# The small matmuls of two mixers: keys in tiles of 72, 72 and 128, matmuls of one array shape side by side

## The chip, the cores and the metric

The kernel runs on one core of a Trainium2 chip. The metric is the time of the program on the device in microseconds (us), from runs of the whole program; a profiled execution of the same program gives the rows that are read below.

## What is computed

A trunk of two layers over 256 frames with 16 learned meta tokens ahead of them, so 272 tokens of 1024 features, all in float32. Every layer adds half a gated feed-forward network, a mixer, and half a second feed-forward network. The parts of the reference that matter here are the mixers:

```python
for layer in range(DEPTH):
    h = h + 0.5 * swiglu(rms_norm(h, ffn1_norm[layer]), ...)
    hn = rms_norm(h, mix_norm[layer])
    y = even_mixer(hn, ...) if layer % 2 == 0 else odd_mixer(hn, ...)
    h = h + y
    h = h + 0.5 * swiglu(rms_norm(h, ffn2_norm[layer]), ...)
return h[:, N_META:]

# even_mixer: 8 indexer heads score the keys, the 64 best keys of each query are kept,
#   8 heads of softmax attention over them; beside it retention with 8 heads:
score = einsum('bqh,bqhs->bqs', iwb, relu(einsum('bqhd,bsd->bqhs', iqb, ik)))
s = einsum('bqhd,bqkhd->bhqk', qb, kg) * dh ** -0.5      # masked, softmax, times v
inner = einsum('bnihd,bnjhd->bnhij', qc, kc) * dmat      # retention: masked, times v
# odd_mixer: 8 heads of windowed attention (2 key heads) with one more score, the sink;
#   beside it a causal mean over 2, 4, 8 and 16 tokens through a 128x128 matrix each
p = softmax(concatenate([s, sink], axis=-1), axis=-1)[..., :-1]
```

## The kernel before

**The stream.** All weights are cut into 128x128 blocks, 2680 of them, packed in the order of their use. Each block is loaded (L138), split into two parts `whi` and `wlo` by ScalarE (L156) and VectorE or GpSimd (L157), and used by three matmuls (`mmw`, L247 to L249) on a moving operand of 272 or 256 token columns. Blocks follow each other in fixed lists of groups (`EV_GROUPS`, `OD_GROUPS` and others); a group's blocks add up in one PSUM bank.

**The work beside it.** What a mixer does with a projection's result (norms, scores, softmax, products) is written as generators, called tasks. A task issues some instructions and yields a number: so many stream blocks are issued before its next step. These numbers stand in the table `W`. So the order on every engine is fixed when the program is built, and each engine takes its instructions in that order. In the mixers a unit of eight blocks is split in two halves of 128x512 (`halves`), one each four blocks.

**Tokens.** Tokens stand in columns, so 272 keys are cut as 128, 128 and 16. A query block is 128 of the 256 frames: the first (`t=0`) sees 144 keys, the second (`t=1`) all 272. Heads stand in pairs in one tile of 128 rows, head `p` on rows 64p to 64p+63.

**The small matmuls**, which are the ones that the change touches:
- The indexer (L573): for 8 heads and 2 query blocks one matmul of 64 rows each, then ScalarE's relu (L575) and VectorE's sum (L578).
- Attention (`attend`): one task for a head pair and a query block, 8 in each mixer. It issues the scores of both heads (L470), their maxima with the mask (L476, VectorE), the exponentials (L480, ScalarE), the division by the sum (L483, L485, VectorE), the turns of the probabilities through TensorE (L493, and L494 for the last 16 keys), copies (L498, L499), and the product with the values (L506, and L507 for the 16 keys) into rows 64p of one bank, head by head.
- Retention (`retain`), once for each of 8 heads: turn of the values (L668), scores (L675 to L677), masks (L680 to L682), and seven blocks later the product (L685 to L687).
- `head_norm` (L433, L436) is the norm of a head's queries or keys. In the odd mixer it waits 15 blocks (`hn_sum`) after the square on ScalarE (L433) before the sum over rows (L436). `norm_r` (L302) is the norm over all features; a mixer's first result waits for it. `pool_mix` (L809 on GpSimd, L813, L816, L819, L821) is the causal mean.

Float32 matmuls of the side work run as two passes; turns run as one. What TensorE's rows call `64*128` is the shape of the stationary operand: rows and columns of the array that the matmul uses.

Of the kernel before, what the change touches and what calls it, by code (L numbers as in the profile page):

```python
# [11 lines left out]
F32 = mybir.dt.float32  # L12
F32R = mybir.dt.float32r
AF = mybir.ActivationFunctionType
# [38 lines left out]
def order_ffn_in0():  # L53
    """The very first phase: in the order in which the tokens are loaded."""
# [13 lines left out]
OD_GROUPS = ([("ck", 0), ("cq", 0), ("cv", 0)] + [("cq", i) for i in (1, 2, 3)] + [("dx", i) for i in (3, 2, 1, 0)])  # L68
# [41 lines left out]
# How many blocks of the weight stream go between the steps of the work beside it.  # L110
W = dict(first_sq=2, hid=6, hid_lo=1, hn_sum=15, hn_out=15, tok=15, tok_out=1, ev=dict(max=1, exp=5, norm=2,
         turn=4, copy=5, pv=6, lo=1), ev_every=(11, 11), od=dict(max=1, exp=4, norm=1, turn=3, copy=1, pv=4,
         lo=1), od_every=(5, 8), ix=10, ix_add=2, top_a=5, top_b=3, meta=4, rope=10, ret_v=1, ret_s=1,
         ret_y=7, ret_sum=7, ret_out=14, ret_lo=2, pool=7, pool_g=8, pool_mm=4, pool_lo=4)


class Weights:
    """The stream of weight blocks: loaded, split into two float32r parts, and handed out in order."""
# [23 lines left out]
    def load_part(self, i):  # L142
        """The first unit in two loads."""
# [8 lines left out]
    def part(self, u, s):  # L152
        """Splits the columns s of unit u."""
# [48 lines left out]
class Trunk:  # L202
# [32 lines left out]
    def table(self, name):  # L235
        """Loads the activation tables of the functions that follow, where one set serves several of them."""
# [15 lines left out]
    def rsqrt(self, out, mean, on=None):  # L252
        """out = (mean + eps) ** -0.5: the table's value and one Newton step; mean may be in PSUM."""
# [16 lines left out]
    def prep_x(self, m, norm, c):  # L270
        """The moving operand of the next projection: h * gain in two float32r parts."""
# [9 lines left out]
    def finish(self, m, ps, coef, norm, c):  # L281
        """h += coef * ps, and what the next norm and projection need of it."""
# [15 lines left out]
    def norm_r(self, c):  # L298
        """The norm's factor per token, on every partition."""
# [9 lines left out]
    def start(self):  # L309
# [9 lines left out]
        # The tensor engine's clock rises once it has been busy for a while: it starts on zeros.  # L319
# [28 lines left out]
    def first_x(self):  # L348
        """The first norm's operand, and the sum of squares that it needs later."""
# [79 lines left out]
    def head_norm(self, raw, gain, pool, tag, bufs, put, c=slice(0, T)):  # L429
        """RMSNorm over the 64 dims of each of the two heads of a tile."""  # L430
# [3 lines left out]
        yield W["hn_sum"]  # L434
# [4 lines left out]
        yield W["hn_out"]  # L439
# [4 lines left out]
    def to_tokens(self, raw, put):  # L444
        """[128 dims, tokens] -> three tiles [tokens, 128 dims] through the tensor engine."""
# [3 lines left out]
        for i, n in ((0, 128), (1, 128), (2, 16)):  # L449
# [536 lines left out]
```

## Time and profile before

| | us |
|---|---|
| median of 3 runs | 1116.1 (1114.81 to 1116.37) |
| span of the profiled execution, first to last instruction | 1113.3 |
| TensorE busy in it | 1104.5 (99%) |
| VectorE busy | 712.1 (64%) |
| ScalarE busy | 523.9 (47%) |
| GpSimd busy | 172.0 (15%) |
| even mixer, its first stream matmul to the next phase's first | 229.9 |
| odd mixer, the same | 83.5 |

The profiled execution gives a span and no time of its own beside it; the runs lie 2.8 us above that span in the median. PE is TensorE's matmuls, PEld its weight loads, DVE VectorE, ACT ScalarE, POOL GpSimd, SP SyncE. A matmul's row has its start and its length; the length holds the way through the array (0.28 us for one of 272 columns, while the next starts 0.13 us after it), so the cost of something between stream matmuls is read from the starts around it.

### The profile page before, as it was taken

Reading aid. Unit: us, or ns where it says so; the run is one execution under the profiler, and the core shown is the slowest. Engines: PE = TensorE matmul, PEld = TensorE weight load, DVE = VectorE, ACT = ScalarE, POOL = GpSimd, SP = SyncE. Lnnn points to the kernel's source line nnn. Section 1 sums busy time; section 2 is a strip of 40 time slices with the busy share of each in tenths; the row PEclk is TensorE's granted clock in tenths of the full one; section 3 lists DMA queues with packets and bytes.
Section 4 is the critical chain, followed back from the end, with each engine's and each line's share of the span. In section 5 each row is a group of like instructions: output and inputs, shape, how many; then the busy total and the mean of one; then the engine's idle time right before and its main releaser. Section 6 shows DMA issues by size and latency. Waiting matters only on the chain.

```text
span 1113.3 us, 20774 instructions
## 1 busy us (share of the span) xinstructions
PE 1104.5 (99%) x8624; PEld 1064.0 (96%) x8624; DVE 712.1 (64%) x1244; ACT 523.9 (47%) x877; POOL 172.0 (15%) x213
## 2 busy tenths in 40 slices
PE   8999999999999999999999999999999999999998
PEld 7999999989889899999999999999999799999998
DVE  5776654559864567776664476665557867777642
ACT  6554434446345455544443354443435546554531
POOL 2000002428430444000001200000113421000000
PEclk9999999999999999999999999999999999999999
DMA  7554544424643225454545445545454225555551
GB/s 269 191 196 182 186 162 183 136 105 152 205 152 125 97 87 184 179 192 159 186 154 189 188 152 189 179 164 189 151 194 165 76 77 181 199 198 184 192 202 40
DMA packets 29533, 183.39 MB, mean 165 GB/s; under 512 B 3648, under 2 KB 6080, under 8 KB 8320
## 3 DMA queue, kind: packets, MB, share of 16 engines
q1 hardware_dynamic: 29184, 181.25, 45.3%
q8 instruction: 67, 1.10, 0.4%
q0 software_dynamic: 256, 0.83, 0.2%
q14 instruction: 26, 0.21, 0.1%
HBM read 179.90 MB, written 1.05 MB: 163 GB/s over the span
## 4 chain that ended last, share of the span: by engine, by line
PE 92%; DVE 5%; ACT 1%; DMA 1%; issue 0%; SPq 0%; DVEq 0%; ACTq 0%
PE mm L247 29%; PE mm L248 28%; PE mm L249 28%; DVE wlo L157 2%; PE sd L506 1%; PE sd L507 1%; PE sd L573 1%; PE sd L470 1%; PE sd L493 1%; DMA raw<-in_w 1%; ACT whi L156 1%; PE sd L675 0%; DVE ev_t L441 0%; DVE isc L587 0%; PE sd L668 0%
## 5 line engine op out<-in xcount | busy, mean ns | idle before, releaser
L247 PE MATMUL mm<-xhi,whi 128*128 128x272 f32 (+1 forms) x1816 | 532.7, 293 | 1.4 <-ACT whi L156 1.3
L249 PE MATMUL mm<-xhi,wlo 128*128 128x272 f32 (+1 forms) x1816 | 521.0, 287 | 1.2 <-DVE wlo L157 1.2
L248 PE MATMUL mm<-xlo,whi 128*128 128x272 f32 (+1 forms) x1816 | 520.6, 287 | 0.2
L157 DVE TENSOR_TENSOR wlo<-raw,whi 128x1024 fp32r<-128x1024 f32 (+1 forms) x394 | 412.2, 1079 | 82.3 <-ACT whi L156 81.9
L156 ACT ACTIVATE whi<-raw 128x1024 fp32r<-128x1024 f32 (+1 forms) x407 | 347.7, 895 | 29.0 <-PE mm L248 22.2
L247 PEld LDWEIGHTS mm<-xhi,whi 128*128 128x128 f32 x1816 | 342.6, 189 | 11.7 <-issue 5.4
L249 PEld LDWEIGHTS mm<-xhi,wlo 128*128 128x128 f32 x1816 | 343.3, 189 | 1.8 <-DVE wlo L157 1.8
L248 PEld LDWEIGHTS mm<-xlo,whi 128*128 128x128 f32 x1816 | 342.2, 188 | 1.4 <-DVE xlo L277 0.6
L249 PE MATMUL mm<-hhi,wlo 128*128 128x272 f32 (+1 forms) x704 | 201.4, 286 | 0.0
L248 PE MATMUL mm<-hlo,whi 128*128 128x272 f32 (+1 forms) x704 | 201.4, 286 | 0.0
L247 PE MATMUL mm<-hhi,whi 128*128 128x272 f32 (+1 forms) x704 | 201.1, 286 | 0.0
L247 PEld LDWEIGHTS mm<-hhi,whi 128*128 128x128 f32 x704 | 132.6, 188 | 0.0
L248 PEld LDWEIGHTS mm<-hlo,whi 128*128 128x128 f32 x704 | 132.5, 188 | 0.0
L249 PEld LDWEIGHTS mm<-hhi,wlo 128*128 128x128 f32 x704 | 132.5, 188 | 0.0
L390 ACT ACTIVATE gr<-gr 128x272 f32<-128x272 f32 (+1 forms) x88 | 37.7, 428 | 153.7 <-DVE gr L388 153.7
L276 ACT ACTIVATE xhi<-h 128x272 fp32r<-128x272 f32 (+1 forms) x48 | 24.6, 520 | 152.6 <-DVE h L285 149.0
L285 DVE SCALAR_TENSOR_TENSOR h<-mm,h 128x272 f32<-128x272 f32 (+1 forms) x48 | 20.7, 432 | 113.8 <-PE mm L249 113.8
L395 ACT ACTIVATE hhi<-ur 128x272 fp32r<-128x272 f32 (+1 forms) x88 | 37.7, 428 | 91.1 <-DVE ur L392 91.1
L292 POOL TENSOR_TENSOR acc<-h 128x272 f32<-128x272 f32 (+1 forms) x5 | 3.2, 635 | 433.9 <-DVE h L285 433.9
L389 DVE TENSOR_TENSOR ur<-mm,r 128x272 f32<-128x272 f32 (+1 forms) x88 | 38.1, 433 | 43.4 <-PE mm L249 43.3
L398 DVE TENSOR_TENSOR hlo<-ur,hhi 128x272 fp32r<-128x272 f32 (+1 forms) x88 | 38.5, 438 | 42.0 <-ACT hhi L395 42.0
L392 DVE TENSOR_TENSOR ur<-gr,ur 128x272 f32<-128x272 f32 (+1 forms) x88 | 38.5, 438 | 14.9 <-ACT gr L390 8.8
(168 smaller groups left out, 889.8 us busy)
## 6 DMA issues: line engine op xcount, KB each, us to landing
raw<-in_w SPq DMA_DIRECT2D x165, 1024.0 KB, 4.8
tab<-in_tab SPq DMA_DIRECT2D x8, 272.0 KB, 4.5
raw<-in_w SPq DMA_DIRECT2D x4, 512.0 KB, 5.9
sw<-ev_t SPq DMA_DIRECT2D x32, 34.0 KB, 2.9
out<-h SPq DMA_DIRECT2D x8, 128.0 KB, 1.7
h<-in_h SPq DMA_DIRECT2D x1, 544.0 KB, 7.4
raw<-in_w SPq DMA_DIRECT2D x2, 256.0 KB, 3.9
h<-in_h SPq DMA_DIRECT2D x1, 272.0 KB, 5.7
```

The lines of the kernel that those rows point to most:

```text
L156: self.nc.scalar.activation(hi[:, s], src[:, s], AF.Copy)
L157: eng.tensor_tensor(lo[:, s], src[:, s], hi[:, s].bitcast(F32), op=OP.subtract)
L247: mm(ps, wh, hi, start=start, stop=False)
L248: mm(ps, wh, lo, start=False, stop=False)
L249: mm(ps, wl, hi, start=False, stop=stop)
L276: nc.scalar.activation(hi[:, c], self.h[m][:, c], AF.Copy, scale=g)
L285: nc.vector.scalar_tensor_tensor(h, ps, coef, h, op0=OP.mult, op1=OP.add)
L389: nc.vector.tensor_tensor(ur[:, c], pu, r, op=OP.mult)
L390: nc.scalar.activation(gr[:, c], gr[:, c], AF.Silu)
L392: nc.vector.tensor_tensor(ur[:, c], gr[:, c], ur[:, c], op=OP.mult)
L395: nc.scalar.activation(hi[:, c], ur[:, c], AF.Copy)
L398: nc.vector.tensor_tensor(lo[:, c], ur[:, c], hi[:, c].bitcast(F32), op=OP.subtract)
```

## The change

Keys are cut in tiles that are never smaller than 72: attention takes 72, 72, 128 (`KEYS`), so that the first query block's 144 keys are the first two; retention takes 128, 72, 72 (`RKEYS`). One attention task serves both query blocks of a head pair: four score matmuls, ten turns and ten value products stand one after another, 4 tasks in each mixer in place of 8. The value products alternate between the two heads. The indexer issues the four score matmuls of a head pair together. Retention's scores leave `retain` for a task of their own (`scores`) that makes both heads of a pair at once, up to four heads ahead. Masks and indexer scores of both query blocks stand in one tile of 416 columns, so relu runs once over 416 columns. The table `W` gets other numbers; the odd mixer's `head_norm` gets its own (`od_hn`: 4 blocks to the sum, 10 to the result), and `OD_GROUPS` mixes the pooling groups with the queries. The rotary tables' buffers go from 3 to 2.

```diff
+KEYS = ((0, 72), (72, 72), (144, 128))
+RKEYS = ((0, 128), (128, 72), (200, 72))
+NKEYS = (144, T)
+QOFF = (0, 144)
...
-OD_GROUPS = ([("ck", 0), ("cq", 0), ("cv", 0)] + [("cq", i) for i in (1, 2, 3)] + [("dx", i) for i in (3, 2, 1, 0)])
+OD_GROUPS = ([("ck", 0), ("cq", 0), ("cv", 0), ("cq", 1), ("dx", 3), ("cq", 2), ("dx", 2), ("cq", 3)]
+             + [("dx", i) for i in (1, 0)])
...
-W = dict(first_sq=2, hid=6, hid_lo=1, hn_sum=15, hn_out=15, tok=15, tok_out=1, ev=dict(max=1, exp=5, norm=2,
-         turn=4, copy=5, pv=6, lo=1), ev_every=(11, 11), od=dict(max=1, exp=4, norm=1, turn=3, copy=1, pv=4,
-         lo=1), od_every=(5, 8), ix=10, ix_add=2, top_a=5, top_b=3, meta=4, rope=10, ret_v=1, ret_s=1,
-         ret_y=7, ret_sum=7, ret_out=14, ret_lo=2, pool=7, pool_g=8, pool_mm=4, pool_lo=4)
+W = dict(first_sq=2, hid=6, hid_lo=1, hn_sum=15, hn_out=15, od_hn=(4, 10), tok=15, tok_out=1,
+         ev=dict(max=1, max2=2, exp=3, exp2=2, norm=2, norm2=2, turn=4, copy=2, pv=4, lo=1), ev_every=22,
+         od=dict(max=1, max2=2, exp=2, exp2=2, norm=1, norm2=1, turn=3, copy=1, pv=3, lo=1), od_every=8,
+         ix=10, ix_relu=1, ix_add=2, top_a=5, top_b=3, meta=4, rope=10, ret_every=10, ret_mask=1, ret_v=1, ret_s=2,
+         ret_sum=7, ret_out=14, ret_lo=2, pool=3, pool_g=3, pool_mm=3, pool_lo=2)
...
+        pss = [self.bank("sd"), self.bank("sd")]
+        for t in range(2):
+            q0 = META + 128 * t
+            for p in range(2):
+                b = slice(64 * p, 64 * p + 64)
+                nc.tensor.matmul(pss[p][:, QOFF[t]:QOFF[t] + NKEYS[t]], qT[b, q0:q0 + 128], kT[b, :NKEYS[t]],
+                                 start=True, stop=True)
...
+        turned = [self.bank("sd") for _ in range(3)]
+        for t in range(2):
+            for p in range(2):
+                for kt in range(2 + t):
+                    k0, n = KEYS[kt]
+                    ps, c = (turned[t], 2 * p + kt) if kt < 2 else (turned[2], p)
+                    nc.tensor.transpose(ps[:n, c * 128:c * 128 + 128], s[:, p, so[t] + k0:so[t] + k0 + n], self.ident)
...
+        ps = self.bank("sd")[:, :SEQ]
+        for t in range(2):
+            for kt in range(2 + t):
+                n = KEYS[kt][1]
+                for p in range(2):
+                    b = slice(64 * p, 64 * p + 64)
+                    v, c = (pt[t], 2 * p + kt) if kt < 2 else (pt[2], p)
+                    nc.tensor.matmul(ps[b, t * 128:t * 128 + 128], v_cols(kt, n, p), v[:n, c * 128:c * 128 + 128],
+                                     start=(kt == 0), stop=(kt == 1 + t))
...
+            def scores():
+
+                for i in range(4):
+                    while i not in got["bq"] or i not in got["bk"] or st["ret"] < 2 * i - 2:
+                        yield 1
+                    q, k = got["bq"][i], got["bk"][i]
+                    pss = [self.bank("sd"), self.bank("sd")]
+                    o = 0
+                    for k0, n in RKEYS:
+                        for p in range(2):
+                            b = slice(64 * p, 64 * p + 64)
+                            nc.tensor.matmul(pss[p][:n, o:o + T - k0], k[b, k0:k0 + n], q[b, k0:T],
+                                             start=True, stop=True)
+                        o += T - k0
+                    yield W["ret_mask"]
+                    for p in range(2):
+                        s1 = mp.tile([128, T], F32, tag="rt1", name="rt1", bufs=4)
+                        s2 = mp.tile([72, 216], F32, tag="rt2", name="rt2", bufs=4)
+                        nc.vector.tensor_tensor(s1, pss[p][:, :T], cau[:, :T], op=OP.mult)
+                        nc.vector.tensor_tensor(s2, pss[p][:72, T:T + 216], cau[:72, T:], op=OP.mult)
+                        kept[2 * i + p] = (s1, s2)
+                        yield 1
+                    yield W["ret_every"]
...
                 y = self.bank("sd")[:, :T]
                 nc.tensor.matmul(y, vb[:, 0, :], s1, start=True, stop=False)
-                nc.tensor.matmul(y[:, 128:T], vb[:, 1, :], s2[:, :144], start=False, stop=False)
-                nc.tensor.matmul(y[:, 256:T], vb[:16, 2, :], s2[:16, 144:160], start=False, stop=True)
+                nc.tensor.matmul(y[:, 128:T], vb[:72, 1, :], s2[:, :144], start=False, stop=False)
+                nc.tensor.matmul(y[:, 200:T], vb[:72, 2, :], s2[:, 144:], start=False, stop=True)
```

How instructions stand now is shown at three places. In these rows `sd` is a PSUM bank of the side work, `mm` one of the stream, `ev_t` a tile of queries or keys, `at_s` the scores, `at_p` and `at_r` the turned probabilities, `vA` the values.

First, TensorE in the even mixer, around the product with the values of a first query block. Before:

```order
L470 MATMUL sd<-ev_t 128x144 x2
L247 MATMUL mm<-xhi,whi 128x272
L248 MATMUL mm<-xlo,whi 128x272
L249 MATMUL mm<-xhi,wlo 128x272
L506 MATMUL sd<-at_p,vA 64x128
L507 MATMUL sd<-at_r,vA 64x128
```

The pair L506, L507 stands a second time after this, for the other head, and then the turns. Now:

```order
L529 MATMUL sd<-at_p_3571,vA 64x128 x4
L529 MATMUL sd<-at_p_3572,vA 64x128 x4
L529 MATMUL sd<-at_p_3573,vA 64x128 x2
L483 MATMUL sd<-ev_t 128x144 x2
L483 MATMUL sd<-ev_t 128x272 x2
L256 MATMUL mm<-xhi,whi 128x272
```

All ten products of a head pair stand together, and the scores of a later pair follow without a stream block between.

Second, TensorE in the even mixer, retention (`rt` is the masked scores, `vb` the turned values, `ones_v` the norm's matrix). Before, the scores of one head:

```order
L249 MATMUL mm<-xhi,wlo 128x272
L675 MATMUL sd<-ev_t 128x272
L676 MATMUL sd<-ev_t 128x144
L677 MATMUL sd<-ev_t 16x16
L247 MATMUL mm<-xhi,whi 128x272
```

Their product (L685 to L687) stands eight blocks after them. Now, at the third head pair:

```order
L258 MATMUL mm<-xhi,wlo 128x272
L699 MATMUL sd<-ev_t 128x272 x2
L699 MATMUL sd<-ev_t 72x144 x2
L699 MATMUL sd<-ev_t 72x72 x2
L256 MATMUL mm<-xhi,whi 128x272
L257 MATMUL mm<-xlo,whi 128x272
L258 MATMUL mm<-xhi,wlo 128x272
L725 MATMUL sd<-rt_4551,vb 128x272
L726 MATMUL sd<-rt_4552,vb 128x144
L727 MATMUL sd<-rt_4552,vb 128x72
```

Here the first product that reads the masked scores stands one block behind them; so it does at the fourth pair, while the first two pairs' scores stand long ahead.

Third, VectorE in the odd mixer, between the maxima and the division by the sum of the first head pair (`od_t` is a projection's result, `ogq` the queries' gain, `hn_r` the head's norm). Now:

```order
L451 SCALAR_TENSOR_TENSOR od_t<-od_t,ogq_9762,hn_r 128x256
L435 TENSOR_TENSOR od_t<-mm,r 128x256
L166 TENSOR_TENSOR wlo<-raw,whi 128x512
L503 RECIPROCAL at_m<-at_m 128x2
L506 TENSOR_SCALAR at_s<-at_s,at_m 128x144 x2
L503 RECIPROCAL at_m<-at_m 128x2
L506 TENSOR_SCALAR at_s<-at_s,at_m 128x272 x2
```

Before, for the first query block of the second pair:

```order
L510 TENSOR_TENSOR oylo<-sd,oyhi 128x128
L157 TENSOR_TENSOR wlo<-raw,whi 128x512
L441 SCALAR_TENSOR_TENSOR od_t<-od_t,ogq_9840,hn_r 128x256
L483 RECIPROCAL at_m<-at_m 128x2
L485 TENSOR_SCALAR at_s<-at_s,at_m 128x144 x2
L474 COPY at_s<-sinks 128x2
```

What divided one query block's two heads now divides both blocks', and the turns come behind all four.

By the same order, TensorE has 8410 instructions before and after, VectorE 1228 and 1203, ScalarE 845 and 829, GpSimd 210 and SyncE 224 both times. The weight blocks are the same ones; in the odd mixer the sum of the first head norm (L436, now L446) stands 5 blocks behind L302 (now L311), where it stood 16 behind it; scores (L483) stand 12 blocks ahead of their turns (L514) in the first three head pairs and 6 ahead in the last.

## Rows read from the trace of the kernel before

**Rows 1.** The profile's page, first part: busy us, share of the span, instructions.
```profile
PE 1104.5 (99%) x8624; PEld 1064.0 (96%) x8624; DVE 712.1 (64%) x1244; ACT 523.9 (47%) x877; POOL 172.0 (15%) x213
```

**Rows 2.** Waits of PE: who waited for whom, us, times, longest.
```profile
PE sd L617 <- DVE ms L613: 0.7, 1, 0.7
PE sd L470 <- DVE od_t L441: 0.6, 1, 0.6
```

**Rows 3.** Busy times in the two mixers: stretch, length, engines, PE clock, DMA.
```profile
208.55:438.44 229.89, 229.24 (x1667) 205.37 (x1666) 156.24 (x383) 114.80 (x264) 94.30 (x109) 1.00 0.38 135
836.76:920.28 83.52, 82.49 (x609) 70.59 (x608) 62.75 (x161) 44.97 (x112) 30.29 (x40) 1.00 0.28 99
```

**Rows 4.** Timeline of PE around one L436: start, us, what, count.
```profile
244.45 0.29 PE L249 MATMUL mm<-xhi,wlo 128*128 128x272 f32 x1
244.58 0.62 PE L436 MATMUL sd<-hn_sq,ones_h 128*128 128x272 f32 x2
...
245.16 0.29 PE L248 MATMUL mm<-xlo,whi 128*128 128x272 f32 x1
```

**Rows 5.** Timeline of PE around one indexer matmul.
```profile
220.60 0.28 PE L249 MATMUL mm<-xhi,wlo 128*128 128x256 f32 x1
220.81 0.72 PE L573 MATMUL sd<-ev_t 64*128 64x272 f32 x2
...
221.69 0.28 PE L248 MATMUL mm<-xlo,whi 128*128 128x256 f32 x1
```

**Rows 6.** Timeline of PE around one pair of score matmuls, two heads.
```profile
309.64 0.29 PE L249 MATMUL mm<-xhi,wlo 128*128 128x272 f32 x1
309.86 0.73 PE L470 MATMUL sd<-ev_t 64*128 64x272 f32 x4
...
310.75 0.29 PE L248 MATMUL mm<-xlo,whi 128*128 128x272 f32 x1
```

**Rows 7.** Timeline of PE: stream matmuls around a second query block's L506, L507.
```profile
346.51 0.29 PE L249 MATMUL mm<-xhi,wlo 128*128 128x272 f32 x1
...
348.83 0.29 PE L248 MATMUL mm<-xlo,whi 128*128 128x272 f32 x1
```

**Rows 8.** Matmuls of L625 that lie in 291.20 to 291.25 and in 291.40 to 291.45.
```profile
291.05 0.40 PE L625 MATMUL sd<-mpt,vA 16*64 16x16 f32 x4
...
291.24 0.41 PE L625 MATMUL sd<-mpt,vA 16*64 16x16 f32 x7
```

**Rows 9.** Stream matmuls around one head's L675 to L677, then around L685 to L668.
```profile
356.86 0.28 PE L249 MATMUL mm<-xhi,wlo 128*128 128x272 f32 x1
...
358.34 0.29 PE L248 MATMUL mm<-xlo,whi 128*128 128x272 f32 x1
...
360.72 0.29 PE L249 MATMUL mm<-xhi,wlo 128*128 128x272 f32 x1
...
362.48 0.29 PE L248 MATMUL mm<-xlo,whi 128*128 128x272 f32 x1
```

**Rows 10.** Timeline at the odd mixer's start: the norm's sum, the first head's square.
```profile
842.29 0.62 PE L302 MATMUL sd<-acc,ones_d 128*128 128x272 f32 x2
...
845.90 0.43 ACT L433 ACTIVATE hn_sq<-od_t 128x272 f32<-128x272 f32 x1 [2.00 <-DVE od_t L426]
```

**Rows 11.** Timeline of DVE and ACT in the odd mixer: steps of the softmax.
```profile
861.54 0.49 DVE L476 CUSTOM_DVE_ANT_0 at_s<-sd,omsk,sinks 128x272 f32<-128x272 f32 x1
...
863.84 0.53 ACT L480 ACTIVATE at_s<-at_s,at_m 128x273 f32<-128x273 f32 x1
...
865.42 1.45 DVE L485 TENSOR_SCALAR at_s<-at_s,at_m 128x272 f32<-128x272 f32 x2
...
887.23 0.63 DVE L485 TENSOR_SCALAR at_s<-at_s,at_m 128x272 f32<-128x272 f32 x2
```

**Rows 12.** Timeline of DVE in the even mixer: half a weight unit, a retention mask.
```profile
357.04 0.69 DVE L157 TENSOR_TENSOR wlo<-raw,whi 128x512 fp32r<-128x512 f32 x1 [0.88 <-ACT whi L156]
...
357.85 0.42 DVE L680 TENSOR_TENSOR rt<-sd,cau 128x272 f32<-128x272 f32 x1
```

More of the change, by code (lines that the diff above doesn't have):

```diff
@@ L427, in evac, with head_norm @@
         return t
-    def head_norm(self, raw, gain, pool, tag, bufs, put, c=slice(0, T)):
+    def head_norm(self, raw, gain, pool, tag, bufs, put, c=slice(0, T), wt=None):
         nc = self.nc
@@ L460, in attend @@
         nc = self.nc
-        q0, nk = (META, 144) if t == 0 else (META + 128, T)
-        ne = nk + (sink is not None)
-        s = pool.tile([128, 2, T + 1], F32, tag="at_s", name="at_s", bufs=2)
-        sm = pool.tile([128, 6], F32, tag="at_m", name="at_m", bufs=3)
-        mn, tot, inv = (sm[:, 2 * a:2 * a + 2] for a in range(3))
-        pss = []
-        for p in range(2):
-            b = slice(64 * p, 64 * p + 64)
-            ps = self.bank("sd")[:, :nk]
-            nc.tensor.matmul(ps, qT[b, q0:q0 + 128], kT[b, :nk], start=True, stop=True)
-            pss.append(ps)
@@ L482, in attend @@
-        yield wt["norm"]
-        nc.vector.reciprocal(inv, tot)
-        for p in range(2):
-            nc.vector.tensor_scalar(s[:, p, :nk], s[:, p, :nk], inv[:, p:p + 1], None, op0=OP.mult)
-        yield wt["turn"]
-        full = t + 1
-        ps = self.bank("sd")
-        rest, o = (self.bank("sd"), 0) if t else (ps, 256)
-        for p in range(2):
-            for kt in range(full):
-                c = (p * full + kt) * 128
-                nc.tensor.transpose(ps[:, c:c + 128], s[:, p, kt * 128:kt * 128 + 128], self.ident)
-            nc.tensor.transpose(rest[:16, o + p * 128:o + p * 128 + 128], s[:, p, full * 128:nk], self.ident)
@@ L508, in attend @@
-        nc.scalar.activation(yhi[:, q0:q0 + 128], ps, AF.Copy)
+        e = int(sinks is not None)
+        so = (0, NKEYS[0] + e)
+        s = pool.tile([128, 2, NKEYS[0] + T + 2 * e], F32, tag="at_s", name="at_s", bufs=2)
+        sm = pool.tile([128, 12], F32, tag="at_m", name="at_m", bufs=3)
+        mn, tot, inv = (sm[:, 4 * a:4 * a + 4] for a in range(3))
+        pss = [self.bank("sd"), self.bank("sd")]
[5 more added lines that the diff above has]
+                                 start=True, stop=True)
@@ new lines, in attend @@
+        for t in range(2):
+            for p in range(2):
+                a, v = 2 * t + p, s[:, p, so[t]:so[t] + NKEYS[t] + e]
+                nc.scalar.activation(v, v, AF.Exp, bias=mn[:, a:a + 1], scale=-1.0, accum_out=tot[:, a:a + 1])
+            yield wt["norm" if t else "exp2"]
+        for t in range(2):
+            h = slice(2 * t, 2 * t + 2)
+            nc.vector.reciprocal(inv[:, h], tot[:, h])
+            for p in range(2):
+                a, v = 2 * t + p, s[:, p, so[t]:so[t] + NKEYS[t]]
+                nc.vector.tensor_scalar(v, v, inv[:, a:a + 1], None, op0=OP.mult)
+            yield wt["turn" if t else "norm2"]
@@ L553, in indexer @@
                 ikw, ik2 = st["ikw"], st["ik2"]
-                iws, sc = [], []
+                iws = []
+                sc = mp.tile([128, 144 + T], F32, tag="isc", name="isc", bufs=1)
+                part = [sc[:, QOFF[t]:QOFF[t] + NKEYS[t]] for t in range(2)]
                 yield W["ix"]
@@ L724, in even @@
                     self.spawn(indexer())
+                    self.spawn(scores())
                 elif name == "iq":
@@ L850, in odd @@
             for m, k in order_od_out():
-                while (st["att"] < 2 * (k + 1)) if k < 4 else (k - 4 not in got["dx"]):
+                while (st["att"] < k + 1) if k < 4 else (k - 4 not in got["dx"]):
                     self.tick()
```

170 lines of the change are left out of this document (81 added, 89 removed).

## The prediction

> **What bounds the kernel now.** I read the busy times first. TensorE is busy 1104.5 of 1113.3 us, 99% [rows 1]; VectorE comes next at 64%. So the time is what TensorE has to do, plus the little that it waits. The list of waits came second: the two longest waits of the mixers' own matmuls are 0.7 us (L617, the meta tokens' division) and 0.6 us (L470, scores) [rows 2], and 1113.3 - 1104.5 = 8.8 us is all that it stands idle, the program's start and end included. Third, the stretches of the two mixers: TensorE's clock is granted at 1.00, the upper level of 2.4 GHz, in both, and VectorE is busy 156 of 230 us (68%) and 63 of 84 us (75%) [rows 3]. A matmul less is therefore time won, until TensorE has to stand for VectorE. How much room there is: the even mixer holds 1272 stream matmuls; at their pitch of about 0.126 us that is 160 of the 229.9 us, so some 69 us are small matmuls; the odd one holds 432, 53 us, and so 30 us.
>
> **How a visit is priced.** A matmul's own length holds its way through the array, so I take the time from the start of the last stream matmul ahead of a visit to the start of the second one behind it, and subtract two pitches (0.13 us each at 272 columns, 0.12 at 256). The sum of the head's norm (L436), two passes of 272 columns in the full shape: 245.16 - 244.45 - 0.26 = 0.45 us [rows 4], 0.23 a pass; in proportion to the columns a pass of 144 is 0.12, of 128 0.107, of 72 0.06. An indexer matmul of the same columns on 64 rows: 221.69 - 220.60 - 0.24 = 0.85 [rows 5]. The 0.39 more is what it costs to leave the full shape and come back. Two heads' scores, four passes, cost the same: 310.75 - 309.64 - 0.26 = 0.85 [rows 6]; so the second head, in the other half of the rows, is free. A second block's products with the values, twelve passes: 348.83 - 346.51 - 0.26 = 2.06 [rows 7]; 12 x 0.107 = 1.28 leaves 0.78 for five changes of shape, 0.156 each.
>
> **The change, part by part, on TensorE.**
>
> Indexer: 8 visits of 272 keys at 0.85 and 8 of 144 keys at 0.85 - 2 x 0.11 = 0.63, together 11.8 us. Now 4 visits with 2 x 0.23 + 2 x 0.12 + 0.39 = 1.09, 4.4 us. -7.5.
>
> Attention's scores: 8 head pairs (4 in each mixer) at 0.85 + 0.63, 11.8 us; now 8 x 1.09 = 8.7. -3.1.
>
> Products with the values: a pair's second block at 2.06, its first with four passes less, 2.06 - 4 x 0.107 = 1.63; 8 x 3.69 = 29.5 us. Now ten products, twenty passes, alternate between the two halves of the columns. Whether such halves run beside each other no wide matmul of this trace shows; the meta tokens' products, also on 64 columns, do: where one head's are issued four lie within a stretch of 0.05 us, where two heads' alternate seven do [rows 8]. I take them as free as the row halves: 10 x 0.107 + 2 x 0.156, rounded up to 1.40, x 8 = 11.2. -18.3. The other end, one after another: 20 x 0.107 + 0.31 = 2.45, x 8 = 19.6, -9.9.
>
> The Trainium skill ("TensorE: Matmul & The Clock Gate", Part 3, packing small matmuls) gives a measured 2.38 times for three column tiles, so less than three. As an estimate from that page, two halves at the same efficiency would gain 1.59 times, a visit would cost 0.28 us more and the whole 2.2 us, a time of about 1093. That halves run beside each other agrees with rows 8; how completely, no row here shows.
>
> Retention's scores: one head is 358.34 - 356.86 - 0.26 = 1.22 [rows 9], x 8 = 9.8 us; now 4 pairs at 2 x (0.23 + 0.12 + 0.06) + 0.39 = 1.21, 4.8 us. -5.0, more than half of it the change to the 16-row piece. Retention's product with the three turns: 362.48 - 360.72 - 0.26 = 1.50 [rows 9], less three turns at 0.11 is 1.17; the 72-row piece in place of 16 rows takes a change of shape away and adds up to 0.1 of columns: 0.92 (0.82 if 72 rows are no other shape than 128, 1.26 if they are), x 8. -2.0 (-2.8 to +0.7). The turns stay at ten for a pair and count nothing.
>
> Sum: -7.5 - 3.1 - 18.3 - 5.0 - 2.0 = **-35.9 us**.
>
> **What TensorE will wait for.** The cover gets thinner in the same edits: 36 us less TensorE work for the same VectorE work, and shorter numbers in the table.
> (a) The odd mixer's first head norm. The norm's sum (L302) starts at 842.29, and the head's square, which waits for it, ends at 845.90 + 0.43 = 846.33 [rows 10]: 4.04 us. The head's sum (now L446) stands only 5 blocks behind it, its own 0.46 and 5 x 0.38 for the blocks, 2.4 us: a wait of 1.7 (1.4 to 2.2), and up to 0.8 at the next head.
> (b) The odd softmax. From scores to turns are 12 blocks, 12 x 0.36 = 4.3 us, and the visits between. The chain is four maxima at 0.49, the last pair's exponentials at 2 x 0.53, the last pair's division at 0.63 while GpSimd rests or 1.45 while it works [rows 11], and a weight half of 0.69 ahead on VectorE [rows 12]: 4.3 to 5.2 us and the handing over between engines; the last pair has 6 blocks, 2.2 us, and the pooling's tail behind it. I take 6.5 for four pairs and tail (3 to 10).
> (c) Retention's third and fourth pair: the product stands one block, 0.38 us and the second head's share, behind the scores; the two masks take 0.42 each at most, with a weight half possibly ahead [rows 12]: 0.5 to 1.6 each, about 3 in all (1 to 3.5).
> (d) The first scores of the even mixer behind rotary work, with two buffers for its tables now in place of three: 0.6 (0 to 0.8).
> (e) The meta tokens and the first unit: 1.4, where before has 0.7 at L617 and some smaller ones.
> Together 13.8 (6 to 20); before's own such waits, 0.7 and 0.6 [rows 2] and smaller ones that I put at 1.6, go: 13.8 - 2.9 = **+10.9 us** (3 to 17).
>
> Counted at nothing: VectorE's instructions fall from 1228 to 1203 and ScalarE's from 845 to 829, GpSimd's and SyncE's don't change, and neither bounds; the wider relu and mask work on the same elements; the larger mask transfer lies long ahead of retention. Without that cover the first masks would be late once, by about a microsecond.
>
> **The sum.** 1113.3 - 35.9 + 10.9 = 1088.3 us for the profiled span; the runs' median lies 2.8 above the span, so **1091 us**. Its own range is 1086 to 1097: the ends of the waits give 1083 and 1097, but the lower one needs all five at their best.
>
> **The rivals.**
> - *Column halves run one after another.* The products give -9.9 in place of -18.3, the sum 1099.5. For it: no wide pair is in the trace. Against it: rows 8 and the free row halves of rows 6.
> - *The waits double.* VectorE and GpSimd get in each other's way on the divisions, as in the 1.45 us of rows 11, in every pair; with 10 more the time is about 1101. For it: VectorE at 75% in the odd mixer, which has to do the same in 75 us. Against it: in the even mixer from scores to turns there are some 20 blocks.
> The Trainium skill ("SBUF — State Buffer") says that VectorE and GpSimd share a port pair that one of them holds alone, for operations with two SBUF inputs or in the faster modes; 1.45 against 0.63 us agrees, and it speaks for this rival.
> - *Pieces of 72 rows are a shape of their own.* Then the change does not do what it says: each visit keeps changes of shape at about 0.16, two in a value product, one or two in a retention visit, 6 to 7 us in all: 1098.
> - *Slower.* One task per pair makes TensorE stand at the turns (L514) through the whole softmax chain of both blocks, about 5 us for each of eight pairs, 40 us: 1113.3 - 35.9 + 40 + 2.8, about 1120. It decides from 4.5 us a pair, that is, if the blocks between scores and turns (4.3 us in the odd, more in the even mixer) covered nothing. They do cover unless VectorE's queue is already that far behind, and at 68 to 75% it isn't.
>
> **Chances.** Forecast 0.72; halves one after another 0.10; waits doubled 0.10; 72 rows a shape 0.04; slower 0.02; a gain that stays out for another reason 0.02. The range from 1086.5 to 1099.5 holds most of the forecast, the first rival in half, and the third. A measurement of this kernel can tell about 0.2% from no change; faster by more than that 0.97, within 0.01, slower 0.02.
>
> **What would show it.** In the changed kernel's trace: a value product visit (L529) of about 1.4 us between stream matmuls, 2.45 if the halves run in turn, 1.7 if 72 rows are a shape; scores (L483, L596) 1.1, retention's scores (L699) 1.2; the even stretch near 206 us, the odd near 75 us. TensorE's waits should add to about 14 us, at L446, L514, L725 and the meta tokens; the forecast is wrong if L514 alone holds over 10 us, or if the visits are right and the stretches are not.

## The result, and the profile after

The changed kernel takes 1097.5 us in the median (1096.24 to 1099.22) where the kernel before takes 1115.7: a ratio of 0.984, 95% interval 0.9825 to 0.9851 (the 1116.1 us shown ahead of the prediction are the median of three of these four runs). The forecast was 1091 us with a range of 1086.5 to 1099.5. So the kernel became faster, as forecast, but by 18 us and not 25, and the time lies near the upper end.

TensorE still sets the time. The first part of the profile's page, busy us, share and instructions, to be read beside [rows 1]:

```profile
PE 1075.1 (98%) x8624; PEld 1053.5 (96%) x8624; DVE 713.5 (65%) x1219; ACT 520.9 (48%) x861; POOL 175.7 (16%) x213
```

Its idle time went from 8.8 to 20.2 us (1095.3 - 1075.1). Where it goes, the waits of TensorE say (who waited for whom, us in total, times, longest), against [rows 2]:

```profile
PE sd L446 <- ACT hn_sq L442: 3.4, 2, 1.8
PE sd L514 <- DVE at_s L506: 2.5, 3, 1.9
PE sd L699 <- POOL ev_t L683: 2.2, 1, 2.2
PE sd L725 <- DVE rt L706: 1.6, 2, 0.8
...
PE mm L256 <- ACT oyhi L858: 1.1, 2, 0.6
...
PE sd L855 <- DVE at_m L503: 0.8, 1, 0.8
```

Before, the longest of the waits of the mixers' own matmuls was 0.7. And the two mixers, each from its first stream matmul to the next phase's first (length, engines' busy time, TensorE's clock, DMA), against [rows 3]:

```profile
209.34:420.18 210.84, 206.55 (x1666) 196.28 (x1665) 159.21 (x366) 112.19 (x252) 98.51 (x109) 0.99 0.42 148
818.52:902.44 83.92, 75.18 (x609) 68.71 (x608) 61.18 (x153) 44.65 (x108) 29.86 (x40) 0.98 0.28 99
```

The even mixer gave 229.89 - 210.84 = 19.1 us. **The odd mixer gave nothing**: 83.52 before, 83.92 now, although TensorE is busy 7.3 us less in it. And in both the mean clock is no longer 1.00. The other phases kept their lengths within 0.1 us, but for the stretch ahead of the even mixer, which differs by up to 1.7 us between the executions of all these kernels.

**The visits came out as priced.** Timeline of TensorE in the changed kernel: the ten value products of a head pair, a pair's indexer scores, retention's scores of a pair, and one product of retention, each with the last stream matmul ahead and the second one behind (start, us, what, count):

```profile
331.28 0.29 PE L258 MATMUL mm<-xhi,wlo 128*128 128x272 f32 x1
331.50 1.31 PE L529 MATMUL sd<-at_p,vA 72*64 72x128 f32 x20
...
332.97 0.29 PE L257 MATMUL mm<-xlo,whi 128*128 128x272 f32 x1
```

```profile
222.94 0.28 PE L258 MATMUL mm<-xhi,wlo 128*128 128x256 f32 x1
...
224.27 0.28 PE L257 MATMUL mm<-xlo,whi 128*128 128x256 f32 x1
```

```profile
310.05 0.29 PE L258 MATMUL mm<-xhi,wlo 128*128 128x272 f32 x1
310.26 1.10 PE L699 MATMUL sd<-ev_t 64*128 64x272 f32 x12
...
311.53 0.29 PE L257 MATMUL mm<-xlo,whi 128*128 128x272 f32 x1
```

```profile
360.16 0.29 PE L258 MATMUL mm<-xhi,wlo 128*128 128x272 f32 x1
360.28 0.68 PE L725 MATMUL sd<-rt,vb 128*128 128x272 f32 x2
...
361.40 0.29 PE L257 MATMUL mm<-xlo,whi 128*128 128x272 f32 x1
```

By the same subtraction of two pitches: 332.97 - 331.28 - 0.26 = 1.43 (forecast 1.40), 1.09 (1.09), 1.22 (1.21), 0.98 (0.92; most others are 0.92). As sums, each visit at its undisturbed price: indexer -7.4, scores -3.1, value products 29.5 - 8 x 1.43 = -18.1, retention's scores -4.9, its products -1.9, together **-35.4 us, forecast -35.9**. So all but 0.5 us of the miss lies in what TensorE waits for, and in its clock.

### The profile page after: what moved, and what is told of

The parts are those of the page before. It is cut to its first block, busy times and chain, and to the rows that moved or that the text cites. A ratio compares the mean times of both kernels' runs of the same rounds, so it can differ in the third digit from the quotient of the medians.

```text
span 1095.3 us, 20703 instructions
## 1 busy us (share of the span) xinstructions
PE 1075.1 (98%) x8624; PEld 1053.5 (96%) x8624; DVE 713.5 (65%) x1219; ACT 520.9 (48%) x861; POOL 175.7 (16%) x213
## 4 chain that ended last, share of the span: by engine, by line
PE 86%; DVE 6%; ACT 3%; DMA 2%; POOL 1%; issue 1%; SPq 0%; POOLq 0%; ACTq 0%; DVEq 0%
PE mm L256 28%; PE mm L257 27%; PE mm L258 27%; DVE wlo L166 3%; ACT whi L165 1%; DMA raw<-in_w 1%; DMA sw<-ev_t 1%; PE sd L529 1%; PE sd L514 1%; ACT rs L268 0%; PE sd L483 0%; ACT at_s L499 0%; ACT rs L269 0%; DVE ev_t L435 0%; PE sd L725 0%
```

## The experiments

Of eleven runs the first four ask for the visits and for the wait at L699, the next three for the clock and for single parts of the change in the kernel before, the last four for the table of numbers.

**Value products head by head.**

```diff
-            for kt in range(2 + t):
-                n = KEYS[kt][1]
-                for p in range(2):
-                    b = slice(64 * p, 64 * p + 64)
+            for p in range(2):
+                b = slice(64 * p, 64 * p + 64)
+                for kt in range(2 + t):
+                    n = KEYS[kt][1]
```

> The changed kernel with the value products (L529) issued head by head and not alternating; the same matmuls otherwise. Theory (the two column halves run beside each other only when they alternate in the queue): a visit goes from 1.43 us to 20 x 0.107 + 0.31 = 2.45, eight of them, +8 us, about 1105. Rival (the visits are short only because the 16-row pieces and their changes of shape are gone): no change, 1097 to 1098.

Measured: 1101.5 us, ratio 0.9873. The visit (same view as above):

```profile
332.34 0.29 PE L258 MATMUL mm<-xhi,wlo 128*128 128x272 f32 x1
332.56 1.58 PE L529 MATMUL sd<-at_p,vA 72*64 72x128 f32 x20
334.30 0.29 PE L257 MATMUL mm<-xlo,whi 128*128 128x272 f32 x1
```

334.30 - 332.34 - 0.26 = 1.70 us: 0.27 more than when they alternate, far less than the 2.45 of one after another. Both expectations fall. The two column halves overlap even head by head, for a good part: the first eight of these passes start in pairs, 0.01 us apart, where in the kernel before, whose halves stand apart by a change of shape, no two start closer than 0.11 us. Alternating gives the rest, 8 x 0.27 = 2.2 us. The run lost 4.0 us, most of what is beyond that in the odd mixer (86.68 us, of which 4 x 0.27 are this edit's); the same changed kernel, run again below, has 85.87 there, so that part is not this edit's.

**Slack ahead of the first retention scores.**

```diff
+                    if i == 0:
+                        yield 8
                     q, k = got["bq"][i], got["bk"][i]
```

> The changed kernel with eight more stream blocks ahead of retention's first score visit, one number. There TensorE stood 2.2 us for GpSimd's rotary work, and the granted clock of the 6 us behind was 0.72. Theory (the visit is issued one block behind GpSimd's instructions, so the order makes the wait; the clock falls because TensorE stood): the visit goes from 4.07 to 1.22 us, the clock stays at 1.00, together -2.9 - 1.1 = -4 us. Rival A (the clock falls for another reason, such as the mixer's small matmuls): -2.9 us and the slow stretch stays. Rival B (GpSimd is late by more than the order): a rest of the wait remains.

**Three buffers for the rotary tables.**

```diff
-            NB = 42
+            NB = 39
...
-                tab = mp.tile([128, 2, T], F32, tag="tab", name="tab", bufs=2)
+                tab = mp.tile([128, 2, T], F32, tag="tab", name="tab", bufs=3)
...
-                sw = mp.tile([128, T], F32, tag="sw", name="sw", bufs=2)
+                sw = mp.tile([128, T], F32, tag="sw", name="sw", bufs=3)
```

> The changed kernel with three buffers for the rotary tables and the swapped halves in place of two, as before the change had; the room comes from three of the 42 buffers of projections' results. GpSimd's idle time ahead of the late rotary step was 3.17 us, ended by the table's transfer. Theory (the scores stand too close behind the rotary work, whatever its buffers): the wait at L699 stays within 0.5 us of 2.2, no change. Rival (two buffers make the transfer late, and GpSimd with it): the wait goes, and the slow clock with it, -3 to -4 us.

Measured: 1095.8 us (0.9816) with slack and 1096.4 us (0.9826) with three buffers, so the slack took 1.7 us off the median and not the 4 expected. The intervals of both ratios overlap with the changed kernel's, so what follows rests on the rows. First the changed kernel itself at this place, TensorE's timeline:

```profile
296.68 0.29 PE L258 MATMUL mm<-xhi,wlo 128*128 128x272 f32 x1
299.19 1.51 PE L699 MATMUL sd<-ev_t 64*128 64x272 f32 x12 [2.22 <-POOL ev_t L683]
...
301.02 0.43 PE L257 MATMUL mm<-xlo,whi 128*128 128x272 f32 x1
301.24 0.43 PE L258 MATMUL mm<-xhi,wlo 128*128 128x272 f32 x1
```

TensorE stands, that is, has nothing to run, 2.22 us for GpSimd's last rotary step. Behind it a stream matmul takes 0.43 and not 0.29 us, and they start 0.22 and not 0.13 us apart. The same six microseconds in the changed kernel, with slack, and with three buffers (the eighth number is the clock; 0.72 is the mean of a part at the upper level, 2.4 GHz, and a part at the lower, 1.2 GHz):

```profile
299.00:305.00 6.00, 5.81 (x39) 5.56 (x40) 4.97 (x10) 0.88 (x3) 3.44 (x5) 0.72 0.61 227
```

```profile
299.00:305.00 6.00, 6.00 (x62) 4.98 (x61) 5.02 (x14) 1.88 (x5) 3.92 (x5) 1.00 0.77 278
```

```profile
299.00:305.00 6.00, 6.00 (x60) 5.85 (x60) 4.43 (x9) 1.49 (x3) 2.58 (x3) 1.00 0.59 224
```

With slack the visit is 1.22 us, the wait is gone, and the even mixer is 207.55 us long, 3.3 less. So the order lets GpSimd's lateness through to TensorE: `got` is filled when GpSimd's instructions are issued, and the scores come one block later. Part of the gain does not reach the whole time: the odd mixer, which the edit does not touch, is 85.12 us long in this execution, 1.2 more, at a mean clock of 0.96. With three buffers the wait is there as before:

```profile
297.85 1.10 PE L699 MATMUL sd<-ev_t 64*128 64x272 f32 x12 [2.24 <-POOL ev_t L683]
```

The rival of the buffers is out. But here **the clock stayed at 1.00 behind nearly the same wait, 2.24 us**. In the changed kernel the fall costs 0.6 us within the visit (4.07 - 1.22 - 2.22) and about 1.0 behind it (ten starts 0.10 us late), and it doesn't follow from the wait alone.

**Retention's keys cut in 128, 128 and 16 again.**

```diff
-RKEYS = ((0, 128), (128, 72), (200, 72))
+RKEYS = ((0, 128), (128, 128), (256, 16))
...
-                nc.tensor.matmul(y[:, 200:T], vb[:72, 2, :], s2[:, 144:], start=False, stop=True)
+                nc.tensor.matmul(y[:, 256:T], vb[:16, 2, :], s2[:16, 144:160], start=False, stop=True)
```

> The changed kernel with retention's keys cut in 128, 128 and 16 again; the scores stay gathered in pairs. Theory (a 16-row piece costs two changes of shape, more than the columns it saves): the product L725 to L727 goes from 0.92 to 1.17, eight times +2.0; the gathered scores from 1.22 to about 1.3, four times +0.3; one more mask on VectorE for each head; +2 to +3 us. Rival (the pieces cost nothing, gathering is all of the gain): the columns fall, -0.5 us or no change.

Measured: 1103.9 us (1101.4 to 1105.9), ratio 0.9897; the even mixer is 214.98 us long, 4.1 more. The products where nothing waits go from 0.92 to 1.21 us (three of the eight), 8 x 0.29 = 2.3 us; the gathered scores from 1.22 to 1.24, next to nothing. The other five products take 1.84 to 2.50 us with what stands beside them, 1.1 us more in all than their matmuls explain: TensorE waits longer for the masks, of which there is a third one for each head (1.9 us in all, 1.6 in the changed kernel), and once for ScalarE's copy of the turned values (0.5 us), which is twice as wide here. The rest is not shown to be this edit's: TensorE stands 3.2 us ahead of the first retention scores here, where two executions of the changed kernel have 2.2 and 2.4. The size of the pieces is a gain apart from gathering, as the theory had it; its price was set too low in part because I counted matmuls only.

**Stands made on purpose, in feed-forward phases.**

```diff
+                if not first and p == 0 and d == KD and j in (2, 7, 12, 17):
+                    ps1, ps2 = self.bank("st1"), self.bank("st2")
+                    s = hp.tile([128, T], F32, tag="stand", name="stand", bufs=2)
+                    nc.tensor.matmul(ps1[:, :T], self.ones_h, self.h[0], start=True, stop=True)
+                    nc.scalar.copy(s, ps1[:, :T])
+                    for _ in range((2, 7, 12, 17).index(j)):
+                        nc.gpsimd.tensor_tensor(s, s, s, op=OP.mult)
+                    nc.tensor.matmul(ps2[:, :T], self.ones_h, s, start=True, stop=True)
```

> The changed kernel with twelve made stands of TensorE in three feed-forward phases, where it has nothing but stream matmuls: a matmul waits for a copy of another matmul's result on ScalarE and 0, 1, 2 or 3 steps of 0.75 us on GpSimd behind it. By the rows of the copies (0.4 us, and up to 0.9 behind a weight half) the stands are about 1, 1.7, 2.5 and 3.3 us, three of each. Nothing of the result is read. Theory (a stand of some 2 us can lower the clock wherever it is, and need not: after the same 2.2 us at L699 the changed kernel fell to 0.72 and the one with three table buffers stayed at 1.00): some of the longer six are followed by a stretch at the lower level for 2 to 4 us, none of the shortest three. Rival (the fall belongs to the mixers' small matmuls): the clock stays 1.00 behind all twelve.

One run was made; it took 1152.3 us. The stands were 1.19 (three times), 1.25, 1.91 (three times), 2.57, 3.54 (three times, within 0.01) and 4.16 us. Three of them in TensorE's timeline (the wait stands in the brackets):

```profile
470.83 0.73 PE L425 MATMUL st<-stand,ones_h 128*128 128x272 f32 x2 [1.19 <-POOL stand L424]
...
504.19 0.73 PE L425 MATMUL st<-stand,ones_h 128*128 128x272 f32 x2 [1.91 <-POOL stand L424]
...
720.19 0.72 PE L425 MATMUL st<-stand,ones_h 128*128 128x272 f32 x2 [1.91 <-POOL stand L424]
```

The two microseconds behind them, behind the stand of 2.57 and behind one of 3.55:

```profile
436.70:438.70 2.00, 2.00 (x8) 1.77 (x9) 1.21 (x2) 1.79 (x2) 0.00 (x0) 0.54 0.42 176
471.00:473.00 2.00, 2.00 (x15) 1.92 (x16) 1.96 (x2) 0.96 (x2) 0.00 (x0) 1.00 0.00 0
504.30:506.30 2.00, 2.00 (x11) 1.92 (x12) 2.00 (x3) 0.30 (x1) 0.00 (x0) 0.71 0.23 29
540.60:542.60 2.00, 1.92 (x6) 1.69 (x7) 1.46 (x2) 0.43 (x1) 0.03 (x1) 0.50 0.64 180
...
720.40:722.40 2.00, 2.00 (x16) 1.92 (x16) 2.00 (x3) 0.20 (x1) 0.00 (x0) 1.00 0.28 33
```

Behind the four stands up to 1.25 us the clock stayed at 1.00. Behind those of 1.91 it fell once in three. Behind all five made stands of 2.57 us and more it fell, to 0.50 to 0.54 in these two microseconds; 0.50 is the lower level. Counted from the waiting matmul to the fortieth stream matmul behind it, a fall cost 1.5 to 2.7 us beyond the stand. The rival falls: the mixers' small matmuls are not needed for it.

But the length of the stand doesn't decide it. The same execution has one more long stand, at retention's first scores (L707 in this run), and behind it the clock stayed at 1.00:

```profile
298.40 1.10 PE L707 MATMUL sd<-ev_t 64*128 64x272 f32 x12 [3.23 <-POOL ev_t L691]
```

```profile
299.00:305.00 6.00, 6.00 (x60) 5.77 (x58) 3.72 (x8) 1.49 (x3) 2.36 (x4) 1.00 0.54 211
```

At this place the clock fell in the changed kernel (2.22 us), in its second run, below (2.39), in the runs with products head by head (2.60) and with 16-row pieces (3.24), and in the one with other numbers in the odd mixer, below (2.17); it stayed with three table buffers (2.24) and here (3.23).

**Two parts of the change, each alone in the kernel before.** First the indexer's scores, four together:

```diff
-                for hd in range(8):
...
+                for i in range(4):
...
                     for t in range(2):
                         q0, nk = META + 128 * t, (144, T)[t]
-                        ps = self.bank("sd")[:, :nk]
-                        nc.tensor.matmul(ps, got["iq"][hd // 2][b, q0:q0 + 128], kk[b, :nk], start=True, stop=True)
...
+                        for p in range(2):
+                            b = slice(64 * p, 64 * p + 64)
+                            pss[p, t] = self.bank("sd")[:, :nk]
+                            nc.tensor.matmul(pss[p, t], got["iq"][i][b, q0:q0 + 128], (ikw, ik2)[p][b, :nk], start=True,
+                                             stop=True)
```

> The kernel before with one part of the change alone: the indexer's four score matmuls of a head pair stand together. Relu and sum keep their form and number. Theory: 16 visits, 11.8 us, become 4 of 1.09, 4.4 us, and no new wait: -7.4 us, 1108 to 1109. Rival (the four banks taken at once, or ScalarE's four relus in a row, make TensorE wait): -4 us or less.

Measured: 1108.6 us, ratio 0.9936 (0.9921 to 0.9951), 7.5 us less than before; the even mixer alone is 222.79 us long, 7.1 less. No new wait at the indexer. The 7.4 us that were priced from two rows hold within the spread of the runs (1107.9 to 1109.0 us).

Then the value products alternating, with their 16-row pieces:

```diff
-        for p in range(2):
-            b = slice(64 * p, 64 * p + 64)
-            for kt in range(full):
+        for kt in range(full):
+            for p in range(2):
...
+        for p in range(2):
+            nc.tensor.matmul(ps[64 * p:64 * p + 64, :], v_cols(full, 16, p), pr[:, p * 128:p * 128 + 128], start=False,
+                             stop=True)
```

> The kernel before with one part of the change alone: its value products alternate between the two heads (first all 128-row pieces, then the two 16-row pieces); the 16-row pieces and the two tasks for a pair stay. Theory (halves run beside each other, and each change of shape costs 0.156): a second block's visit goes from 2.06 to 6 x 0.107 + 3 x 0.156 = 1.11, a first one's from 1.63 to 4 x 0.107 + 0.47 = 0.90, eight of both: -13.4 us, about 1102.5. Rival (issued head by head with 72-row pieces the visit was only 0.27 us longer, so alternating brings little and the pieces were what cost): two changes of shape less for each visit, 16 x 0.31 = -5, and 8 x 0.27 = -2, about 1109.

Measured: 1104.4 us, ratio 0.9901 (0.9885 to 0.9918), 11.7 us less. A second block's visit, to be read against [rows 7]:

```profile
341.75 0.29 PE L249 MATMUL mm<-xhi,wlo 128*128 128x272 f32 x1
341.96 0.66 PE L505 MATMUL sd<-at_p,vA 128*64 128x128 f32 x8
342.55 0.43 PE L508 MATMUL sd<-at_r,vA 16*64 16x128 f32 x4
...
343.15 0.29 PE L248 MATMUL mm<-xlo,whi 128*128 128x272 f32 x1
```

343.15 - 341.75 - 0.26 = 1.14 us in place of 2.06; the theory had 1.11. What is missing to 13.4 lies in the odd mixer, 78.65 us long, which gave 4.9 and not 6.7 us. Read with the first run it says: alternating *or* larger pieces takes most of the 18.1 us of the value products. Larger pieces head by head take 8 x (3.69 - 1.70) = 15.9, alternating with the old pieces about 13; they don't add up, since the halves overlap for a good part in both. And these two small edits on the old table, each in a run of its own, give 7.5 + 11.7 = 19.2 us, as much as the whole change; they were not run together.

**The table of numbers.** In the even mixer:

```diff
+W.update({'ret_s': 5, 'meta': 6})
+W["ev"].update({'max2': 3, 'exp': 4, 'copy': 1, 'pv': 5})
...
-                    while i not in got["bq"] or i not in got["bk"] or st["ret"] < 2 * i - 2:
+                    while i not in got["bq"] or i not in got["bk"] or st["pv"] < 2 * i - 2:
                         yield 1
+                    if i == 0:
+                        yield 8
...
+                st["pv"] += 1
```

> The changed kernel with other numbers in the even mixer alone: eight blocks ahead of the first retention scores, a pair's scores let in as soon as the products of the pair two before are issued (not when their results are written), and ret_s 5, meta 6, max2 3, exp 4, copy 1, pv 5. Theory (the waits there are set by the table): L699's 2.9 us, about 1.1 of slow clock and 2 us at L725 go: -5 to -6 us against the changed kernel, 1091 to 1092. Rival (VectorE is full, and a wait taken away comes back behind it): -3 or less.

In the odd mixer:

```diff
-OD_GROUPS = ([("ck", 0), ("cq", 0), ("cv", 0), ("cq", 1), ("dx", 3), ("cq", 2), ("dx", 2), ("cq", 3)]
-              + [("dx", i) for i in (1, 0)])
+OD_GROUPS = [('ck', 0), ('cq', 0), ('cq', 1), ('cq', 2), ('cq', 3), ('cv', 0), ('dx', 1), ('dx', 3), ('dx', 2), ('dx', 0)]
...
+W.update({'od_hn': (12, 9), 'od_every': 7, 'pool_g': 6})
+W["od"].update({'exp': 4, 'exp2': 1, 'lo': 2})
```

> The changed kernel with other numbers in the odd mixer alone: all queries ahead of values and pooling groups, 12 blocks to a head norm's sum and 9 to its result, od_every 7, pool_g 6, exp 4, exp2 1, lo 2. Theory: 3.7 us at L446, 3 at the last tiles' turns and the pooling's tail, and the slow clock behind that tail go in part: -6 to -8 us, about 1090. Rival (the odd mixer has become VectorE's, 62 busy of the 73 us that TensorE's matmuls would take, and waits only move): -2 or less.

Both, and the changed kernel again beside them:

> Both sets of numbers together. Theory: the two add up, -11 to -14 us against the changed kernel, about 1085. Rival: they don't (a shared start or clock effect), 1088 or more.

> The changed kernel again, on the chip of these runs, for comparison. Theory: 1096 to 1099 as before, the wait of 2.2 us at L699 and those of the odd mixer in the same places; the stretches of slow clock may lie elsewhere or be missing, since the same wait had them or not.

| | median, us | ratio to before (interval) | even mixer, us | odd mixer, us |
|---|---|---|---|---|
| changed kernel again | 1098.4 | 0.9852 (0.9838 to 0.9867) | 211.03 | 85.87 |
| even numbers | 1093.1 | 0.981 (0.9796 to 0.9825) | 204.75 | 86.5 |
| odd numbers | 1090.3 | 0.9781 (0.9764 to 0.9797) | 210.4 | 77.84 |
| both | 1084.2 | 0.9729 (0.9714 to 0.9743) | 205.02 | 77.83 |

Each set acts in its own mixer, -6 and -8 us, and together they give -14.2. About 2 of the 8 are slow clock that this execution of the changed kernel has beyond the first one (85.87 us at a mean of 0.94, 83.92 at 0.98). The matmuls are the same in all four. So the theory holds: these waits were those of the table, the order of the groups and the condition on `pv`, not the price of gathering. With both sets the mixers' rows and the longest waits that are left read:

```profile
208.64:413.66 205.02, 204.57 (x1667) 195.04 (x1665) 157.81 (x366) 112.52 (x252) 96.39 (x109) 1.00 0.43 151
811.97:889.80 77.83, 73.64 (x609) 68.31 (x608) 61.80 (x153) 44.10 (x108) 31.23 (x40) 0.98 0.31 106
```

```profile
PE sd L860 <- DVE py L857: 2.7, 2, 2.1
...
PE mm L259 <- DVE oylo L865: 1.2, 1, 1.2
...
PE sd L516 <- DVE at_s L508: 0.7, 2, 0.4
```

The even mixer has no wait of half a microsecond left in its own matmuls; VectorE is busy 77% of it. In the odd one the pooling's tail still makes TensorE stand. At 1084.2 us this version is faster than both kernels, by 30 us in the case of the kernel before.

## Why the prediction was right, and where it was too low

**What bounds, and the visits: right.** TensorE sets the time, and -35.4 us of matmul work stand against -35.9. The term on which most hung, the column halves, was right in size: 1.43 us for 1.40. The estimate from the Trainium skill ("TensorE: Matmul & The Clock Gate", Part 3), 0.28 us more for a visit, was not seen: 20 passes took 1.43 - 0.31 = 1.12 us, 1.9 times faster than 20 x 0.107. That estimate, the rival of halves in turn (2.45 us) and the rival of 72 rows as a shape of their own (1.7 us) are all out by the same row. It takes the row: by the time alone, 1097.5 us, the rival of 72 rows (1098) would have fitted better than the forecast.

**The waits: too low.** By one of its own signs, visits right and stretches not, this part of the forecast failed: the mixers took 210.8 and 83.9 us where it named 206 and 75. The 75 doesn't follow from its own terms either: 83.5 - 10.7 for the visits + 8.8 for (a) and (b), less about 1 of waits that stood before, is about 81, and the even mixer comes to 208 in the same way. So each mixer is about 3 us longer than the terms give. Forecast were 13.8 us of waits; what the visits took beyond their undisturbed price adds to 17.5, and the starts that a slow clock made late behind them to about 2.1 more:

| step of the prediction | forecast, us | measured, us |
|---|---|---|
| (a) head norms, odd mixer (L446: 2.33 - 0.44, 2.46 - 0.44) | 2.3 | 3.9 |
| (b) odd softmax and pooling tail (L514 3.6, L483 0.6, L855 3.4) | 6.5 | 7.6 |
| (c) retention's third and fourth pair (L725 2.1, L717 0.3) | 3.0 | 2.4 |
| (d) first scores behind rotary work (L699: 4.07 - 1.22, of which 2.22 wait) | 0.6 | 2.9 |
| (e) meta tokens, first turns | 1.4 | 0.7 |
| slow clock behind these visits (1.0 behind L699, 1.1 in the odd mixer) | 0 | about 2.1 |
| sum | 13.8 | about 19.6 |

With this, 1113.3 - 35.4 + 19.6 - 2.9 = 1094.6; the profiled span is 1095.3. They agree to about a microsecond, not better: the 2.9 is the forecast's own figure, and the stretch ahead of the even mixer is 0.8 us longer in this execution. The terms that were too low, then, are (d) by 2.3 us, (a) by 1.6, (b) by 1.1, and the clock by 2.1.

**(a)** had one wait right: at the first head norm I forecast 1.7 us, and L446 took 1.9 beyond its price. The second wait was forecast for the next head norm, which waited for nothing; it came at the third, by another mechanism. The chain in the timeline, on VectorE, ScalarE and TensorE:

```profile
835.96 0.48 DVE L451 SCALAR_TENSOR_TENSOR od_t<-od_t,ogq,hn_r 128x256 f32<-128x256 f32 x1 [1.11 <-POOL hn_r L277]
836.36 0.41 DVE L435 TENSOR_TENSOR od_t<-mm,r 128x256 f32<-128x256 f32 x1
...
836.81 0.42 ACT L442 ACTIVATE hn_sq<-od_t 128x256 f32<-128x256 f32 x1 [4.07 <-DVE od_t L435]
...
837.28 0.70 PE L446 MATMUL sd<-hn_sq,ones_h 128*128 128x256 f32 x2 [1.77 <-ACT hn_sq L442]
```

VectorE's instruction for one query tile (L451) stood 1.11 us for GpSimd's norm: 10 blocks were left to it (15 before), and GpSimd had the norm ahead of it in hand until 833.4. Behind L451 in VectorE's queue stood the next projection's result (L435), for which ScalarE's square and then TensorE waited. I had priced the shorter number to the *sum* for the first norm only, and the shorter number to the *result* not at all: a wait put into a queue is paid by what is queued behind it. It takes both numbers. The run with the odd mixer's numbers has 9 blocks to the result, and VectorE stands there too:

```profile
837.83 0.94 DVE L452 SCALAR_TENSOR_TENSOR od_t<-od_t,ogq,hn_r 128x256 f32<-128x256 f32 x1 [0.78 <-POOL hn_r L278]
```

But with 12 blocks to the sum in place of 4, TensorE waits at none of its head norms.

**(d)** named the right resource, GpSimd's rotary work. Only retention's queries and keys go through it, so the first scores behind it are L699. The size was too low, and the reason it gave was the wrong one: with three buffers for the tables the wait is 2.24 us, as with two. What lets it through is the distance of one block; eight blocks more take it away. In the order I had looked for the masks behind these scores, not for the rotary work ahead of them.

**The clock** was counted at 1.00 throughout, since before it was 1.00 in both mixers. Two stretches fell: behind L699, and in the odd mixer at the pooling's tail:

```profile
872.50:875.50 3.00, 1.47 (x6) 0.78 (x5) 2.29 (x10) 1.27 (x5) 0.00 (x0) 1.00 0.00 0
875.50:878.50 3.00, 2.30 (x11) 1.88 (x10) 1.69 (x6) 2.00 (x6) 0.00 (x0) 0.68 0.00 0
878.50:881.50 3.00, 3.00 (x22) 2.89 (x22) 0.87 (x2) 1.08 (x3) 0.00 (x0) 0.75 0.02 5
```

TensorE is busy half of the first three microseconds, and at 0.68 and 0.75 of its clock in the next six. Ahead of this fall there is no single long stand but three short ones of 0.56, 0.83 and 0.56 us. The longest of them:

```profile
875.05 0.67 PE L855 MATMUL sd<-py,dmix 128*128 128x256 f32 x2 [0.83 <-DVE at_m L503]
```

**The rival "the waits double"** was half right in size: the waits came to 1.3 times the forecast, 1.4 with the slow clock. Its mechanism was not seen: the sixteen divisions of the odd mixer took 5.7 us on VectorE before and 5.3 now, and other numbers in the table, with the same instructions, took most of the waits away. The even mixer, where I had trusted 20 blocks between scores and turns, indeed waits little there. That the change makes the kernel slower is out, with 18 us between.

**Open.** Why GpSimd started the late rotary step 3.17 us late (the profile names the table's transfer) is not settled: with three buffers it idles 3.15 us. What decides whether the clock falls behind a stand is not either. And why the odd mixer of the same kernel took 83.92 us in one execution and 85.87 in another is seen only as the mean clock of the stretch, 0.98 and 0.94.

## What to carry to other kernels

Price a small matmul visit by its changes of array shape first (here 0.3 to 0.4 us for leaving the stream's shape and returning, about 0.16 for each one between), then by its columns; a piece of 72 rows can be cheaper than one of 16. When such edits take work from the busiest engine, the distances in its schedule shrink with it: for every consumer count the blocks to its producer on *every* engine, and for every wait what is queued behind it. Of 35 us won here, 17 went into waits and a slower clock, and other numbers in the table gave 14 of them back.

## What was not expected of the hardware

A stand of TensorE can cost more than its length. In the run with made stands the granted clock stayed at 1.00 behind four of 1.25 us and less, fell behind one of three of 1.91 us, and fell to about 0.5 behind all five of 2.57 us and more, where 1.5 to 2.7 us more were lost. It isn't a matter of length alone: behind 3.23 us at another place of the same execution it stayed at 1.00, behind waits of 2.2 us at one place it fell in one kernel and not in another, and in the changed kernel's odd mixer it fell behind three waits of 0.56 to 0.83 us close together. And two column halves of 64 overlap even when one head's products are all issued ahead of the other's in a block of queries: 1.70 us against 1.43 alternating, where one after another would be 2.45.
